# A hybrid decoder layer on one core: scratch places kept free ahead of loads, a corrected booking of products, and a new order of heads

## Chip, core and metric

The kernel runs on one core of a Trainium2 chip. The metric is the device time in microseconds (us) of one execution. The engines are named as the profile names them: PE multiplies matrices (PEld is its weight load), DVE works on vectors, ACT evaluates functions and copies, POOL fills and copies, SP issues the DMAs. Each engine takes its own instructions in the order in which they stand in the program, and waits for the others through semaphores.

## What is computed

One layer of a decoder for 272 prompt positions (16 learned ones and 256 given) and 32 sample positions (8 sequences of 4): 304 columns in all, called T. The reference, cut down:

```
xn = rms_norm(x, norm_mix)
z = xn @ w_in                        # 2048 -> 3360 (RWKV group) + 4096 (retention group)
o_a, S_a = rwkv7_mixer(z[..., :3360], ...)     # 16 heads of 64, state per head 64x64
o_b, S_b = retention_mixer(z[..., 3360:], ...) # 4 heads of 256, state per head 256x256
h = x + concat([o_a, o_b]) @ w_out
hn = rms_norm(h, norm_ffn)
h = h + (silu(hn @ w_gate) * (hn @ w_up)) @ w_down   # 2048 -> 5632 -> 2048
y = rms_norm(h, norm_final)          # meta positions dropped
```

The old states of the eight sample sequences (`state_rwkv`, `state_ret`) are read, and the new ones written.

## The kernel before

**Products.** Activations lie transposed: 128 features in the partitions, the positions in the free dimension. Each weight block of 128x128 is loaded in float32 (tile `wr`, 128x512, that is four blocks, 256 KB; five such buffers), split into a rounded part `wh` (cast on ACT) and a rest `wl` (subtraction on DVE), and multiplied in the single-pass type `float32r` with activations that are split in the same way (`xh`, `xl`): three PE instructions a block, written `acc<-xh,wh`, `acc<-xl,wh`, `acc<-xh,wl`, with 288, 290 or 304 columns. One `wr` tile therefore feeds 12 PE instructions. All weights lie in one stream `big` in the order of use.

**Stages.** First the input projection: three low-rank tiles, then for each of 8 pairs of RWKV heads (`p0` to `p7`) three tiles, for each of 4 retention heads (`r0` to `r3`) six, and for each gate (`g0` to `g3`) two. Then the output projection in two halves (`out`), the first of which needs the results of all 8 pairs, the second those of the retention heads; then the feed-forward part (from about 661 us to the end). While the products of the input run, the recurrences of the heads run as *streams*: Python generators (`pair`, `sample`, `by_token`, `ret` and others), each of which issues a few instructions and yields. They use small float32 products that go to other PSUM banks (`mm`).

**Order.** Nothing is scheduled on the chip: `Plan` walks the program once as a draft with booked durations, decides when a stream's next step is put between the products of the main stream, and the second walk emits the instructions in that order. `Plan.array` books PE's products; `Plan.book` books all others and keeps a clock for each engine. `ORDER` is the order of the heads in the input projection; `AHEAD` and `RAHEAD` say how many pairs and retention heads may be projected before earlier ones have begun; `RSTART[h]` names the pair whose end retention head h waits for; the rank with which a stream is added decides who goes first (`1 + p` for pair p, `20 + h` for retention head h; smaller goes first).

**Scratch.** All other tiles lie in two arenas in SBUF, `arena_dt.float` and `arena_dt.float32r` (so the trace names all of them alike). `Room` notes for each tile from when to when the draft uses it, and `Room.place` packs them, so that tiles of different times share a place. It tries to leave a gap of up to 2000 ns between the last use of a place and the next tile's first, and takes less where the room is short. Where a tile takes over a place, its first instruction waits for the last of the place's users. Tiles that a DMA fills are: `lora` (128x256, 128 KB, two for each pair), `s0w` (a pair's old states, 256 KB, twice for each pair), `s0r` (old retention states, 512 KB, four for each head, again four later for heads 2 and 3), `rmask` (one for each retention head) and `xT` (the residual, four loads of 576 KB in `out`).

**The DMA queue.** Loads of `wr`, loads of scratch tiles and all stores are issued by SP, one after the other. SP waits for each in its turn.

Of the kernel before, what the change touches and what calls it, by code (L numbers as in the profile page):

```python
# [47 lines left out]
WS = 5  # L48
PAIRS = 3
PMAX = 4  # L50
AHEAD = 2
RETS = 2
HELD = 2
RAHEAD = 3
RSTART = (-1, -1, 6, 6)
ORDER = "p0 p1 p2 r0 p3 p4 r1 p5 p6 p7 r2 r3 g0 g1 g2 g3"


PV = {}
# [22 lines left out]
KEYS = ((0, META, SEQ, 0), (P, P, NP - P, SEQ), (LASTK, 2 * P, T - 2 * P, SEQ + NP - P))  # L82
RMW = SEQ + NP - P + T - 2 * P
ROOM = 33008
WIDE = 4800
FREE, GAPS, TRIES = 800.0, (2000.0, 1000.0, 500.0, 200.0, 50.0, 0.0), 12


# [233 lines left out]
class Plan:  # L322
# [53 lines left out]
    def book(self, eng, what, a, k):  # L376
# [13 lines left out]
        n = math.prod(out.shape[1:])  # L390
        if eng == "PE":
            done = self.array(what, *a[:3], at) + 170
        elif eng == "SP":
            self.clock[eng] = at = max(self.clock[eng] + 400, at)
            self.dma = max(self.dma, at + 1400) + 4 * out.shape[0] * n / 320
            done = self.dma + 600
        else:
            each = sum(math.prod(x.shape[1:]) == 1 for x in ins) if n > 1 else 0
            if eng == "DVE":
                big = max(math.prod(x.shape[1:]) for x in aps)  # L400
                per = 0.56 if what == "tensor_scalar" and ins[0].name not in self.banks else 1.05
                dur, tail = {"stream_shuffle": (62 + 1.05 * n, 90), "transpose": (95 + 1.02 * n, 80), "tensor_reduce": (40 + 1.8 * big, 85),
                             "tensor_tensor_scan": (65 + 2.1 * n, 85)}.get(what, (62 + per * n + 67 * each, 83))
            elif eng == "ACT":
                dur, tail = 108 + 0.83 * n + 90 * each - 40 * (ins[0].name in self.banks), 94
            else:
                dur, tail = (60 + 0.85 * n, 60) if what == "memset" else (125 + 0.8 * n, 65) if what == "tensor_copy" else (185 + 1.65 * n, 60)
# [8 lines left out]
            done = at + tail  # L416
        for x in aps:
            for room in self.rooms.values():
                room.use(x, self.count, self.begun if eng == "PE" else self.clock[eng] - 400, done)
        for name in {x.name for x in aps if x.name in self.left}:  # L420
            self.left[name] -= 1
            assert self.left[name] >= 0, name
# [33 lines left out]
    def array(self, what, out, w, x, ready):  # L456


        n, m, k = math.prod(x.shape[1:]), math.prod(w.shape[1:]), w.shape[0]
        up = lambda v: 32 if v <= 32 else 64 if v <= 64 else 128  # L460
        mode, part = (up(k), up(m)), (w.start_partition(), out.start_partition())
        least = 110 if m > 64 else 58
        if w.dtype == F32R:
            mode = up(k), 128
            dur = max(0.417 * n + 13, 107)
        elif what == "transpose":
            dur = max(0.833 * n + 3, least)
        else:
            dur = 2 * max(0.833 * n + 3, least)
        if mode != self.mode:  # L470
            self.mode, self.parts, self.empty = mode, {}, self.clock["PE"] + 90
        at = max(self.parts.get(part, self.empty), self.begun + 5)
        self.idle += max(0.0, ready - at)
        if ready > at + 20 and w.dtype != F32R:
            dur += 90
        at = max(at, ready)
        self.begun = at
        self.parts[part] = at + dur
        self.clock["PE"] = max(self.parts.values())
        return at + dur  # L480
# [126 lines left out]
class Step:  # L607
# [389 lines left out]
    def pair_jobs(self, p):  # L997
# [10 lines left out]

        need = lambda: p < AHEAD or ("go", p - AHEAD) in self.done
        return [self.z_job(3 + 3 * p + j, post(n, 3 + 3 * p + j), need if j == 0 else None,  # L1010
# [466 lines left out]
    def ret_jobs(self, h):  # L1477
# [3 lines left out]
        r = {}  # L1481
# [23 lines left out]
        def v_post(e):  # L1505
            def f(acc):
                if e == 0:
                    r[2] = self.t([P, 2, T], "rv")
                dve.tensor_mul(r[2][:, e, :], acc[:, :T], self.rstd1)
                yield  # L1510
                if e:
                    self.plan.add(self.ret(h, r[0], r[1], r[2]), 20 + h)
            return f

        need = lambda: h < RAHEAD or ("rgo", h - RAHEAD) in self.done
        jobs = []
# [471 lines left out]
```

## Time and profile before

| what | value |
|---|---|
| median of 3 runs | 1567.01 us (1562.27 to 1572.35) |
| the profiled execution | 1565.75 us, of which its span 1563.9 us |
| PE busy | 1511.4 us (97%), 11438 instructions |
| PEld busy | 1480.9 us (95%) |
| DVE, ACT, POOL busy | 1092.1 us (70%), 881.5 us (56%), 31.5 us (2%) |
| moved by DMA | 258.57 MB, mean 165 GB/s |
| mean granted clock of PE | 0.992 |

The ends of PE's instructions are modelled in the profile, so that a busy PE isn't PE at its peak; idle time of PE and a row's count of instructions say more. "PE mm L317 <- ACT" in the rows on waits reads: PE's instruction that writes an `mm` tile waited, and ACT's instruction ended the wait. All instructions are recorded by one helper, line 317, so the rows are told apart by tiles and by time. "SPq" is the waiting of the DMA queue itself.

### The profile page before, as it was taken

The page shows a single profiled execution, that of the slowest core. Times are in us where ns is not written, and L with a number is a line of the kernel's source. Part 1 is how long each engine was busy: PE and PEld are TensorE (multiplying, and loading weights), DVE is VectorE, ACT ScalarE, POOL GpSimd, SP SyncE. Part 2 cuts the span into 40 slices and gives each one's busy share as a digit, 9 for nine tenths or more (in the row PEclk, how much of TensorE's full clock was granted, in tenths as well). Part 3 has the DMA queues.
Part 4 walks back from the last instruction along what each step waited for, and adds up shares of the span by engine and source line. Part 5 has one row for each costly group of instructions (what it writes and reads, how often), then busy time and mean ns, then how long its engine had stood idle before and what let it go on. Part 6 is the DMA issues. An engine that isn't in the chain of part 4 may idle for free.

```text
span 1563.9 us, 32063 instructions
## 1 busy us (share of the span) xinstructions
PE 1511.4 (97%) x11438; PEld 1480.9 (95%) x11438; DVE 1092.1 (70%) x2768; ACT 881.5 (56%) x2109; POOL 31.5 (2%) x165
## 2 busy tenths in 40 slices
PE   8999999999999998998999999999999999999997
PEld 7999899989899997898999999999999999999997
DVE  5988998797889755876665656565656566565657
ACT  6777678676677864556744444444444444444445
POOL 0000010000000000000000000000000000000000
PEclk9999999999999999999999999999999999999999
DMA  6454453354343345874765555555556555566554
GB/s 225 142 161 135 145 166 104 125 165 146 104 146 110 108 126 193 302 260 136 225 185 170 175 169 169 170 175 168 168 171 175 168 176 166 169 173 175 164 174 129
DMA packets 138784, 258.57 MB, mean 165 GB/s; under 512 B 16256, under 2 KB 22656, under 8 KB 138624
## 3 DMA queue, kind: packets, MB, share of 16 engines
q1 hardware_dynamic: 138624, 256.52, 53.6%
q8 instruction: 91, 1.49, 0.4%
q14 instruction: 69, 0.57, 0.1%
HBM read 242.18 MB, written 14.28 MB: 164 GB/s over the span
## 4 chain that ended last, share of the span: by engine, by line
PE 82%; DVE 6%; ACT 4%; DMA 4%; issue 2%; SPq 1%; DVEq 0%; ACTq 0%
PE acc L317 72%; PE mm L317 10%; DVE arena_dt.float L317 4%; ACT arena_dt.float L317 3%; DVE wl L317 2%; DMA arena_dt.float<-s0r 1%; ACT wh L317 1%; DMA wr<-big 1%; DMA arena_dt.float<-lora 1%; SPq L317 1%; DVE xl L317 0%; DVE arena_dt.float32r L317 0%; DMA arena_dt.float<-s0w 0%; DMA arena_dt.float<-xT 0%; ACT arena_dt.float32r L317 0%
## 5 line engine op out<-in xcount | busy, mean ns | idle before, releaser
L317 PE MATMUL acc<-xh,wh 128*128 128x288 f32 (+2 forms) x2592 | 782.9, 302 | 3.8 <-ACT wh L317 3.0
L317 PE MATMUL acc<-xh,wl 128*128 128x288 f32 (+2 forms) x2592 | 765.5, 295 | 2.9 <-DVE wl L317 2.8
L317 PE MATMUL acc<-xl,wh 128*128 128x288 f32 (+2 forms) x2592 | 761.3, 294 | 0.0
L317 ACT CAST wh<-wr 128x512 fp32r<-128x512 f32 (+1 forms) x827 | 501.0, 616 | 338.9 <-PE acc L317 268.3
L317 DVE TENSOR_TENSOR wl<-wr,wh 128x512 fp32r<-128x512 f32 (+1 forms) x827 | 560.3, 685 | 161.0 <-ACT wh L317 155.7
L317 PEld LDWEIGHTS acc<-xh,wh 128*128 128x128 f32 x2592 | 487.3, 188 | 8.7 <-ACT wh L317 4.5
L317 PEld LDWEIGHTS acc<-xh,wl 128*128 128x128 f32 x2592 | 486.2, 188 | 4.9 <-DVE wl L317 4.4
L317 PEld LDWEIGHTS acc<-xl,wh 128*128 128x128 f32 x2592 | 487.2, 188 | 3.1 <-issue 1.9
L317 PE MATMUL acc<-arena_dt.float32r,wh 128*128 128x288 f32 x1408 | 272.7, 292 | 0.2 <-DVE arena_dt.float L317 0.2
L317 PEld LDWEIGHTS acc<-arena_dt.float32r,wh 128*128 128x128 f32 x1408 | 223.7, 188 | 0.4 <-DVE arena_dt.float L317 0.4
L317 PE MATMUL acc<-arena_dt.float32r,wl 128*128 128x288 f32 x704 | 205.6, 292 | 0.0
L317 PE MATMUL mm<-arena_dt.float 128*128 128x128 f32 (+7 forms) x1120 | 171.2, 310 | 27.9 <-ACT arena_dt.float L317 11.2
L317 PEld LDWEIGHTS mm<-arena_dt.float 128*128 128x128 f32 (+1 forms) x1120 | 140.8, 184 | 43.5 <-issue 23.5
L317 DVE TENSOR_TENSOR arena_dt.float<-acc,arena_dt.float 128x288 f32<-128x288 f32 (+4 forms) x181 | 72.7, 419 | 153.3 <-PE acc L317 149.6
L317 DVE TENSOR_TENSOR arena_dt.float<-arena_dt.float 128x32 f32<-128x32 f32 (+23 forms) x658 | 159.2, 279 | 16.3 <-ACT arena_dt.float L317 6.6
L317 ACT ACTIVATE arena_dt.float<-arena_dt.float 128x288 f32<-128x288 f32 (+7 forms) x229 | 97.1, 432 | 106.5 <-DVE arena_dt.float L317 104.6
L317 DVE TENSOR_TENSOR arena_dt.float<-arena_dt.float,acc 128x288 f32<-128x288 f32 (+1 forms) x210 | 94.3, 450 | 78.9 <-PE acc L317 77.7
L317 PEld LDWEIGHTS acc<-arena_dt.float32r,wl 128*128 128x128 f32 x704 | 132.1, 188 | 0.0
L317 ACT COPY arena_dt.float<-mm 64x64 f32<-64x64 f32 (+11 forms) x338 | 95.0, 290 | 47.3 <-PE mm L317 36.0
L317 ACT CAST arena_dt.float32r<-arena_dt.float 128x288 fp32r<-128x288 f32 (+6 forms) x117 | 49.7, 430 | 93.9 <-DVE arena_dt.float L317 83.0
L317 ACT COPY arena_dt.float<-arena_dt.float 128x8 f32<-128x8 f32 (+8 forms) x267 | 62.4, 282 | 32.4 <-DVE arena_dt.float L317 27.8
L317 DVE TENSOR_TENSOR arena_dt.float32r<-arena_dt.float,arena_dt.float32r 128x288 fp32r<-128x288 f32 (+6 forms) x116 | 51.7, 448 | 5.1 <-ACT arena_dt.float32r L317 4.5
(68 smaller groups left out, 578.5 us busy)
## 6 DMA issues: line engine op xcount, KB each, us to landing
wr<-big SPq DMA_DIRECT2D x823, 256.0 KB, 2.9
arena_dt.float<-s0r SPq DMA_DIRECT2D x24, 512.0 KB, 4.5
out_rts<-arena_dt.float SPq DMA_DIRECT2D x16, 512.0 KB, 4.9
arena_dt.float<-s0w SPq DMA_DIRECT2D x16, 256.0 KB, 2.6
arena_dt.float<-xT SPq DMA_DIRECT2D x4, 576.0 KB, 4.1
arena_dt.float<-lora SPq DMA_DIRECT2D x16, 128.0 KB, 2.6
out_rws<-arena_dt.float SPq DMA_DIRECT2D x8, 256.0 KB, 4.3
out_y<-arena_dt.float SPq DMA_DIRECT2D x7, 288.0 KB, 2.4
```

Of the source, the lines that this page charges most:

```text
L317: return self._plan.keep(f(*a, **k))
```

## The change

The diff, without the parts that only move lines:

```diff
-AHEAD = 2
+AHEAD = 4
 RETS = 2
 HELD = 2
-RAHEAD = 3
-RSTART = (-1, -1, 6, 6)
-ORDER = "p0 p1 p2 r0 p3 p4 r1 p5 p6 p7 r2 r3 g0 g1 g2 g3"
+RAHEAD = 2
+RSTART = (-1, -1, 6, 5)
+RRANK = (20, 21, 22, 2.5)
+ORDER = "p0 p1 p2 r0 p3 p4 r1 g0 p5 p6 g1 p7 r2 g2 g3 r3"
...
-WIDE = 4800
+WIDE = 4288
...
         for x in aps:
             for room in self.rooms.values():
-                room.use(x, self.count, self.begun if eng == "PE" else self.clock[eng] - 400, done)
+                room.use(x, self.count, self.begun if eng == "PE" else self.clock[eng] - (8000 if eng == "SP" else 400), done)
...
         if w.dtype == F32R:
             mode = up(k), 128
-            dur = max(0.417 * n + 13, 107)
+            dur = max(0.417 * n + (9 if n == 288 else 11.5), 107)
...
-                    self.plan.add(self.ret(h, r[0], r[1], r[2]), 20 + h)
+                    self.plan.add(self.ret(h, r[0], r[1], r[2]), RRANK[h])
```

A tile that SP loads now counts as in use from 8000 ns (before: 400 ns) ahead of the booked issue of its load, so `Room.place` looks for a place whose last user is done by then. A single-pass product of 288 columns is booked at 129.1 ns (before 133.1), others 1.5 ns shorter than before. The float32r arena may take 4288 elements a partition (before 4800), and the float32 arena gets what is left of 33008. Gates are projected between pairs, retention head 3 last of all; it may begin after pair 5 (before: pair 6), and its stream goes ahead of all pairs but the first two. The set of instructions of each engine stays the same: 10841 on PE, 2650 on DVE, 2111 on ACT, 954 on SP, 169 on POOL.

What this does to the order shows at three places. The first is SP's queue at the load of the states of pair 1 (`s0w`), in the input projection; the names in brackets are the engines (or DMA queues) whose semaphore the row waits for. Before:

```order
L317 DMA wr_1473<-big 128x512 [waits DMAHW6_49,DVE_49]
L317 DMA wr_1492<-big 128x512 [waits DMAHW7_49,DVE_49]
L317 DMA arena_dt.float_73<-s0w 128x512 [waits DVE_49]
L317 DMA wr_1517<-big 128x512 [waits DMAHW0_49,Activation_49]
L317 DMA wr_1539<-big 128x512 [waits DMAHW1_49,Activation_49]
```

The changed kernel:

```order
L318 DMA wr_1510<-big 128x512 [waits DMAHW0_49,DVE_49]
L318 DMA wr_1530<-big 128x512 [waits DMAHW1_49,DVE_49]
L318 DMA arena_dt.float_73<-s0w 128x512
L318 DMA wr_1558<-big 128x512 [waits DMAHW2_49,DVE_49]
L318 DMA wr_1578<-big 128x512 [waits DMAHW3_49,DVE_49]
```

The load stands at nearly the same place in the queue, but no longer waits for DVE: the last user of its place is 138 PE instructions earlier in the program, where before it was the same step of the pair's own stream. Of the 64 loads of scratch tiles, 49 stood before within 60 PE instructions after the last use of their place, and 26 within 10; now 18 and 7 do.

The second place is SP's queue where the input projection ends and `out` begins: the old states (`s0r`) of retention heads 2 and 3. Before:

```order
L317 DMA arena_dt.float_73<-s0r 128x1024 [waits DMAHW3_49,Pool_49]
L317 DMA arena_dt.float_73<-s0r 128x1024 [waits DMAHW4_49]
L317 DMA arena_dt.float_73<-s0r 128x1024 [waits DMAHW5_49,DMAHW1_49,PE_49]
L317 DMA arena_dt.float_73<-s0r 128x1024 [waits DMAHW6_49,DMAHW2_49,PE_49]
L317 DMA arena_dt.float_73<-s0r 128x1024 [waits DMAHW7_49,DMAHW3_49,PE_49]
L317 DMA arena_dt.float_73<-s0r 128x1024 [waits DMAHW4_49,DMAHW0_49,PE_49]
L317 DMA wr_8040<-big 128x512
```

The changed kernel:

```order
L318 DMA arena_dt.float_73<-s0r 128x1024 [waits DVE_49,DMAHW5_49,PE_49,Activation_49]
L318 DMA arena_dt.float_73<-s0r 128x1024 [waits DMAHW6_49]
L318 DMA arena_dt.float_73<-s0r 128x1024 [waits DMAHW7_49]
L318 DMA arena_dt.float_73<-s0r 128x1024 [waits DMAHW0_49]
L318 DMA arena_dt.float_73<-s0r 128x1024 [waits DMAHW1_49,Pool_49]
L318 DMA arena_dt.float_73<-s0r 128x1024 [waits DMAHW2_49,Pool_49]
L318 DMA arena_dt.float_73<-xT 128x4x288 [waits DMAHW5_49,PE_49,DMAHW6_49,Activation_49,Pool_49]
```

Before, the second four loads waited for PE's products of the same two heads, into whose places they went. Now one wait for an engine that has a near user is left among them, the first row's, for the last steps of pair 6.

The third place is PE at the same point. `mm` rows of 128x128 by `cst` are transposes of retention heads; 32x256 is a product with the old states; the rows of 128x288 with `float32r` are the last products of a pair; the first `acc` row opens `out`. Before:

```order
L317 MATMUL acc_7876<-xh_75,wl_7769 128x288
L317 MATMUL mm_1945_7913<-arena_dt.float_73 128x256 x2
L317 MATMUL mm_1954_7941<-arena_dt.float_73 128x256 x6
L317 MATMUL mm_1955_7954<-arena_dt.float_73 128x256 x6
L317 MATMUL mm_1956_7962<-arena_dt.float32r 128x288 x4
L317 MATMUL mm_1959_7968<-arena_dt.float_73 32x256 x8
L317 MATMUL mm_1964_7981<-arena_dt.float_73 32x256 x8
L317 MATMUL mm_1975_8033<-arena_dt.float_73 128x256
L317 MATMUL acc_7876<-xh_75,wh_7790 128x288
```

The changed kernel:

```order
L318 MATMUL acc_7784<-xh_75,wl_7788 128x304
L318 MATMUL mm_1926_7894<-arena_dt.float_73 128x128 x8
L318 MATMUL mm_1931_7909<-cst_323,arena_dt.float_73 128x128 x4
L318 MATMUL mm_1936_7936<-arena_dt.float32r 128x288 x4
L318 MATMUL mm_1943_7955<-arena_dt.float32r,sums_326 128x288 x2
L318 MATMUL mm_1948_7974<-arena_dt.float32r,sums_326 128x288 x2
L318 MATMUL mm_1956_7984<-arena_dt.float_73 32x256 x8
L318 MATMUL mm_1975_8054<-arena_dt.float32r 128x288 x4
L318 MATMUL mm_1982_8080<-arena_dt.float_73 32x256 x8
L318 MATMUL acc_8100<-xh_75,wh_7817 128x288
```

(Rows between these are left out.) Before, the last weight products of the input ran until only the four last products of pair 7 were left, and 76 instructions of heads 2 and 3 and of pair 7 stood between them and `out`. Now 102 stand there, among them the whole end of pair 7, from its eight output products (`mm_1926`) over its two sums (`sums`) to its last four products (`mm_1975`), with head 3 between them; part of head 2 has moved behind the start of `out`.

## Prediction

> **What bounds the kernel now.** I read the page first:
>
> ```profile
> PE 1511.4 (97%) x11438; PEld 1480.9 (95%) x11438; DVE 1092.1 (70%) x2768; ACT 881.5 (56%) x2109; POOL 31.5 (2%) x165
> ```
>
> PE bounds the kernel: its instructions stay the same, so only the time in which it stands still, or runs slowly, can change: 1563.9 - 1511.4 = 52.5 us. The Trainium skill ("Trainium Kernel Development and Optimization", Performance Expectations) says that weight-load busy time, not matmul busy time, tells the distance from the limit. By that the room is 1563.9 - 1480.9 = 83.0 us; the row shows both, and I use the smaller one below, as what a wait can surely give back.
>
> Next, where it stands still, by stretches (columns: length, busy time of each engine with its instructions, granted clock, DMA share, GB/s):
>
> ```profile
> core 0: us, PE busy (x) PEld busy (x) DVE busy (x) ACT busy (x) POOL busy (x), PEclk, DMA share, GB/s
> ...
> 100.00:200.00 100.00, 93.90 (x700) 89.57 (x698) 90.29 (x382) 66.38 (x200) 5.78 (x30) 1.00 0.47 152
> 200.00:300.00 100.00, 95.29 (x723) 93.15 (x722) 82.79 (x253) 78.08 (x236) 5.47 (x28) 1.00 0.38 116
> 300.00:400.00 100.00, 93.93 (x688) 89.43 (x687) 83.48 (x296) 74.59 (x217) 4.43 (x25) 0.98 0.48 152
> 400.00:500.00 100.00, 93.86 (x698) 92.24 (x697) 89.49 (x354) 67.14 (x200) 6.60 (x32) 0.98 0.38 120
> ...
> 576.20:587.10 10.90, 10.90 (x82) 9.35 (x84) 7.00 (x18) 6.42 (x19) 0.21 (x1) 1.00 0.25 98
> 587.10:598.20 11.10, 7.03 (x45) 2.55 (x36) 1.29 (x3) 0.44 (x2) 0.00 (x0) 0.70 0.73 263
> 598.20:602.10 3.90, 3.90 (x30) 3.75 (x29) 0.00 (x0) 1.66 (x4) 0.00 (x0) 0.98 0.03 6
> 602.10:661.00 58.90, 53.42 (x390) 51.56 (x390) 50.27 (x104) 33.85 (x73) 0.00 (x0) 1.00 0.75 253
> ...
> 722.00:775.00 53.00, 47.47 (x318) 42.51 (x317) 31.28 (x61) 39.26 (x129) 1.38 (x7) 1.00 0.53 167
> 775.00:1500.00 725.00, 725.00 (x5627) 725.00 (x5626) 437.60 (x786) 313.28 (x547) 0.00 (x0) 1.00 0.59 173
> ```
>
> From 775 us on PE never waits: 5627 instructions in 725 us, 128.8 ns each. The change leaves that part alone. PE's idle time lies in the input projection (6.1 + 4.7 + 6.1 + 6.1 = 23.0 us from 100 to 500 us), at the turn to `out` (587 to 598 us), in `out` (5.5 us from 602 to 661) and where the late new states of the pairs run beside the first feed-forward products (5.5 us from 722 to 775).
>
> Then what PE waits for there, and what SP did just before. Each pair of rows below is one short window, in order of time (103 to 118, 168 to 180, 277 to 296, 322 to 333, 357 to 369, 408 to 424, 424 to 433, 485 to 496 us): first PE's wait, then SP's (us in total, times, longest):
>
> ```profile
> PE mm L317 <- ACT arena_dt.float L317: 1.6, 1, 1.6
> SPq L317 <- DVE arena_dt.float L317: 8.7, 2, 7.2
> ...
> PE mm L317 <- issue: 1.5, 1, 1.5
> SPq L317 <- ACT arena_dt.float L317: 5.8, 1, 5.8
> ...
> PE mm L317 <- POOL arena_dt.float L317: 1.4, 1, 1.4
> PE mm L317 <- ACT arena_dt.float L317: 0.9, 1, 0.9
> SPq L317 <- DVE arena_dt.float L317: 19.8, 2, 11.2
> ...
> PE mm L317 <- issue: 0.9, 1, 0.9
> SPq L317 <- ACT arena_dt.float L317: 9.0, 1, 9.0
> ...
> PE mm L317 <- ACT arena_dt.float L317: 2.4, 1, 2.4
> SPq L317 <- DVE arena_dt.float L317: 8.1, 1, 8.1
> ...
> PE mm L317 <- DVE arena_dt.float L317: 2.3, 1, 2.3
> SPq L317 <- DVE arena_dt.float L317: 9.6, 2, 7.2
> ...
> PE mm L317 <- issue: 1.2, 1, 1.2
> SPq L317 <- DVE arena_dt.float L317: 10.5, 1, 10.5
> ...
> PE mm L317 <- issue: 1.1, 1, 1.1
> SPq L317 <- ACT arena_dt.float L317: 5.4, 1, 5.4
> ```
>
> This is what to see: PE's rows name ACT, DVE, POOL or nothing ("issue"), but ahead of each stall SP stood 5 to 11 us at one scratch load, because the place that it fills was still in use. Everything behind it in the queue came late: five `wr` tiles in a burst, or a `lora` tile. Then ACT, which casts both in its order, waited for the landing, and with it the small copies that PE needed:
>
> ```profile
> ACT wh L317 <- DMA wr<-big: 4.1, 1, 4.1
> ...
> ACT arena_dt.float32r L317 <- DMA arena_dt.float<-lora: 3.4, 1, 3.4
> ```
>
> The first is from 408 to 424 us, the second from 424 to 433. Five `wr` tiles hold 5 x 12 products, 7.7 us at 128.8 ns: about as long as SP stood.
>
> **Term 1, these eight stalls.** They sum to 1.6 + 1.5 + 2.3 + 0.9 + 2.4 + 2.3 + 1.2 + 1.1 = 13.3 us. Two of them cost more than their length:
>
> ```profile
> 368.00:374.00 6.00, 5.00 (x26) 5.01 (x27) 3.31 (x10) 3.95 (x16) 0.00 (x0) 0.72 0.96 325
> 423.00:429.00 6.00, 5.98 (x37) 5.98 (x38) 5.27 (x21) 5.36 (x17) 0.21 (x1) 0.72 0.00 0
> ```
>
> Right after the stalls of 2.4 and 2.3 us the granted clock has a mean of 0.72 over 6 us: (1 - 0.72) x 6 = 1.7 us of PE's work each, 3.4 us. (The Trainium skill, "TensorE: Matmul & The Clock Gate", HAM oscillation, has PE's clock fall only after idle gaps above about 3.4 us. By that rule these two stalls would leave the clock alone and this term would be 3.4 us less; the two rows show that 2.3 us was enough here.) So 16.7 us hang on blocked loads. Of the loads within 10 PE instructions after their place's last use 7 of 26 remain (within 60, 18 of 49), so I leave 30% of the stalls: a gain of **11.7 us**, between 0 and 16.7. What hides a load then is the distance itself. What is late next is ACT and DVE at their own work, which is rival A.
>
> **Term 2, the turn to `out`.** Around 587 us SP shows one wait:
>
> ```profile
> SPq L317 <- PE mm L317: 11.2, 1, 11.2
> ```
>
> This is the second four `s0r` loads, 2 MB, which could go out only when PE had read the first ones. PE then had nothing else: from 587.1 to 598.2 us it ran 45 instructions, and at clock 0.70. The same kind ran before at this rate:
>
> ```profile
> 585.61 1.93 PE L317 MATMUL mm<-arena_dt.float 128*32 128x256 f32 x32
> ```
>
> 45 of them are 2.7 us, so 11.1 - 2.7 = 8.4 us are lost. In the new order the wait for PE on these loads is gone, but for one row, behind the end of pair 6. Against that, pair 7's end now has no weight products beside it. From its eight output products to its last four lies a chain of some 17 dependent steps on ACT and DVE, each of about 0.44 us; with 0.1 us to hand over that is 9 us (an estimate from rows of the next kind):
>
> ```profile
> 579.15 0.44 ACT L317 ACTIVATE arena_dt.float<-arena_dt.float 128x288 f32<-128x288 f32 x1
> ```
>
> Between these two PE has 24 transposes and most of head 3 and a part of head 2. From the 10.9 us that a like set took from 576.2 to 587.1, less what has moved behind, more the transposes, I estimate 13 us of PE work. So the chain fits, if ACT and DVE serve it at once; they also have the copies of heads 2 and 3. I charge 3 us for that: a gain of **5.4 us**. Bounds: 8.4 if nothing of the chain shows; -3 in rival B.
>
> **Term 3, `out`.** 58.9 - 53.4 = 5.5 us idle. SP's longest wait stands at the residual's load:
>
> ```profile
> SPq L317 <- DVE xl L317: 15.5, 1, 15.5
> ```
>
> The changed kernel still waits for PE at this load, the eight `s0r` loads of the held heads come a little earlier, and the bytes are the same in a stretch with the DMA engines at 0.75. I take half, **2.7 us**, between 0 and 5.5.
>
> **Term 4, the late states.** 53.0 - 47.5 = 5.5 us idle, and
>
> ```profile
> SPq L317 <- PE mm L317: 18.9, 5, 5.1
> ```
>
> Of the eight `s0w` loads here four still wait for PE in the new order (before, five did), but between a transpose and the 128x512 product that follows, 33 to 42 weight products stand in most cases, where 27 to 30 stood. Eight more are 1 us each. I take half: **2.8 us**, between 0 and 5.5.
>
> **Term 5, the rest.** From 100 to 500 us 23.0 - 13.3 = 9.7 us of idle time are not tied to loads. The new order deals these waits anew. It also has more distance for tiles that no DMA writes: 32 of them, before 127, are within 10 PE instructions after another engine's use of their place. The shorter booking puts 4 ns more cover on each 288-column product: in 48 such products 0.2 us, no term of its own. I take **2 us**, from -8 to +8: a new order may bring as many waits as it takes away, but hardly twice as many.
>
> **Sum.** 11.7 + 5.4 + 2.7 + 2.8 + 2 = 24.6 us. The profiled execution took 1565.75 us, 1.9 us beside its span, and 1.3 us less than the median shown. 1565.75 - 24.6 = **1541 us**, 1.6% faster. About 1% is what a measurement of this kernel can tell from no change: below 1551 us is faster, above 1583 us slower. With all terms at their best (16.7 + 8.4 + 5.5 + 5.5 + 8 = 44.1) it is 1522 us.
>
> **Rival A: ACT and DVE take over the stalls (about 1556 us, within 1%).** DVE is busy for 90.3 of the 100 us from 100 to 200, and 89.5 from 400 to 500. PE's work there would come faster while DVE's stays, so a blocked load may only have been the last of several late things. If half of terms 1 and 3 is real and the others give nothing but 3 us of the turn, the sum is 5.9 + 1.4 + 3 = 10 us. Against it: ACT's waits for `wr` and `lora` name the DMA itself. Here too belongs that the change doesn't do what it says: the 8000 ns are a wish that gives way where the room is short, and 18 loads still stand near. That gives the same size. Chance 0.24.
>
> **Rival B: the end of pair 7 stands bare (slower).** Before, the chain from the eight output products (563.7 us) to the last four (584.8 us) took 21.1 us, with 12.5 us of full PE work beside its first half. If it takes 21.1 us again, as ACT and DVE first serve head 3, whose stream now goes ahead of pair 7's, PE stands for 21.1 - 13 = 8 us, in gaps that halve the clock as after the stalls above (two at 1.7 us), and term 2 is -3 us, not +5.4. By itself that makes only 1549 us. It ends on the slower side if the same rank does so all through pairs 5 to 7, which head 3's weight products must cover: the bare chain and the waits of term 5 at -8, and terms 1, 3 and 4 at nothing, is 1565.75 + 3 + 8 = 1577 us or somewhat more. The point from which it decides: terms 1, 3 and 4 below 11 us together. Chance 0.06, half of that over the 1% line.
>
> **How the numbers follow.** The forecast has 0.70: faster by over 1%, between 1522 and 1551 us. Rival A has 0.24 and B 0.06. The range must leave out no more than 0.2: from 1524 us, where nearly all terms are at their best (some 0.06 lies below), to 1561 us, which takes in A's value with half of its own spread (some 0.12 lies above). Faster by over 1%: 0.70, within 1%: 0.26, slower: 0.04.
>
> **What would show it.** Term 1: between 100 and 500 us SP's waits for `arena_dt.float` fall to a third, ACT's waits for `wr` to a few us, PE's idle time from 23 to about 11 us, no clock below 1. Term 2: PE's idle time between the last input product and `out` under 4 us, and no wait for `s0r`; if A is right, PE's waits name ACT and DVE with no SP wait before them, and their sum stays above 16 us. If B is right, the stretch before `out` holds long waits of PE for ACT or DVE, with a halved clock. The prediction is wrong if blocked loads vanish and PE's idle time doesn't.

## The result

The changed kernel takes **1528.26 us** (median of 4, 1527.69 to 1529.31), the kernel before took 1567.37 us beside it (median of 4, 1562.27 to 1572.35). The ratio is 0.9751, 95% interval 0.972 to 0.9783: 39 us faster, where the forecast was 25 us, to 1541. The profiled execution took 1529.31 us, with a span of 1527.4. The helper that records every instruction is line 318 now. Where some executions of a kernel took over 1.5% longer than its fastest, its ratio is that of the others, and its median that of all.

The row of the changed kernel's page that answers to that of before, the busy times:

```profile
PE 1496.6 (98%) x11438; PEld 1474.8 (97%) x11438; DVE 1086.4 (71%) x2768; ACT 884.1 (58%) x2109; POOL 30.6 (2%) x165
```

PE's idle time went from 52.5 us to 1527.4 - 1496.6 = 30.8 us, 21.7 less. Its busy time went from 1511.4 to 1496.6 us, 14.8 less, with the same instructions.

Both profiles hold 11438 rows of PE, so a stretch that counts the same number of them ends at the same place of the work, but for what the new order has swapped around that place. I cut both spans after 100, 3701, 4801 and 5738 instructions of PE; one that lies across a cut is counted on both sides (columns: stretch, length, busy time and count of PE, PEld, DVE, ACT, POOL, granted clock, DMA share, GB/s). The kernel before:

```profile
0.00:22.90 22.90, 18.22 (x100) 15.55 (x101) 13.37 (x28) 15.52 (x32) 0.60 (x8) 0.93 0.81 262
22.90:529.80 506.90, 483.62 (x3603) 469.76 (x3601) 434.32 (x1535) 364.36 (x1065) 28.03 (x146) 0.99 0.44 136
529.80:686.70 156.90, 147.27 (x1102) 138.91 (x1102) 107.01 (x228) 93.57 (x225) 1.46 (x4) 0.98 0.63 215
686.70:819.90 133.20, 127.67 (x939) 122.71 (x939) 87.51 (x167) 80.26 (x207) 1.38 (x7) 1.00 0.60 182
819.90:1563.90 744.00, 734.59 (x5702) 734.00 (x5700) 449.93 (x814) 327.79 (x584) 0.00 (x0) 1.00 0.57 169
```

The changed kernel:

```profile
0.00:19.90 19.90, 16.02 (x100) 14.37 (x101) 12.68 (x27) 14.36 (x30) 6.13 (x41) 1.00 0.87 280
19.90:503.20 483.30, 474.64 (x3603) 466.07 (x3602) 431.70 (x1533) 362.62 (x1054) 21.78 (x114) 1.00 0.49 146
503.20:650.30 147.10, 143.91 (x1103) 137.90 (x1102) 107.14 (x231) 95.40 (x238) 1.36 (x3) 1.00 0.67 220
650.30:783.00 132.70, 127.19 (x940) 122.32 (x939) 87.38 (x167) 79.77 (x207) 1.31 (x7) 1.00 0.61 185
783.00:1527.40 744.40, 734.88 (x5702) 734.09 (x5700) 447.53 (x814) 331.99 (x584) 0.00 (x0) 1.00 0.58 169
```

So the 36.5 us between the spans are 3.0 at the start, **23.6 in the input projection** (506.9 to 483.3), **9.8 at the turn and in `out`** (156.9 to 147.1), 0.5 where the late states run, and nothing in the rest of the feed-forward stage (-0.4). In the projection PE's idle time fell from 23.3 to 8.7 us, by 14.6, and the busy time of its instructions by 9.0. The granted clock explains some 6.6 of the 14.8 us of busy time. Before, it cost (1 - 0.93) x 22.9 = 1.6 us at the start, 3.4 us after two stalls and (1 - 0.70) x 11.1 = 3.3 us at the turn; in the changed kernel one stretch is left, (1 - 0.83) x 10 = 1.7 us. Where the rest of the busy time went is not shown.

The stretches of the input projection that answer to those of before:

```profile
100.00:200.00 100.00, 94.64 (x707) 90.53 (x705) 91.03 (x374) 68.57 (x203) 2.98 (x16) 1.00 0.49 152
200.00:300.00 100.00, 99.68 (x756) 97.68 (x757) 85.26 (x286) 79.53 (x239) 6.48 (x33) 0.99 0.48 149
300.00:400.00 100.00, 97.88 (x755) 96.31 (x754) 92.63 (x308) 78.60 (x232) 6.18 (x33) 1.00 0.45 135
400.00:500.00 100.00, 99.15 (x772) 98.95 (x771) 93.57 (x397) 71.38 (x212) 4.96 (x27) 1.00 0.48 137
```

PE stands idle for 5.4 + 0.3 + 2.1 + 0.9 = 8.7 us there, before 23.0. DVE is busier than before in all four (91.0, 85.3, 92.6 and 93.6 against 90.3, 82.8, 83.5 and 89.5): it gets more done in the same time, and hasn't become the limit. What PE still waits for in these 400 us:

```profile
PE mm L318 <- ACT arena_dt.float L318: 4.2, 4, 2.8
PE mm L318 <- issue: 3.7, 3, 2.1
PE mm L318 <- DVE arena_dt.float L318: 0.6, 1, 0.6
```

These are 8 waits with 8.5 us. The kernel before had 23 with 22.5 us there.

The waits behind it, from 100 to 500 us. Of the kernel before, SP's waits for scratch tiles, and ACT's for landings (us in total, times, longest):

```profile
SPq L317 <- DVE arena_dt.float L317: 164.6, 60, 11.2
...
SPq L317 <- ACT arena_dt.float L317: 30.7, 9, 9.0
...
ACT wh L317 <- DMA wr<-big: 17.9, 8, 4.1
ACT arena_dt.float32r L317 <- DMA arena_dt.float<-lora: 7.8, 4, 3.4
```

Of the changed kernel:

```profile
SPq L318 <- DVE arena_dt.float L318: 150.1, 72, 8.0
...
SPq L318 <- ACT arena_dt.float L318: 11.4, 4, 7.9
...
ACT arena_dt.float32r L318 <- DMA arena_dt.float<-lora: 7.8, 4, 3.0
```

ACT's wait for late `wr` tiles, 17.9 us in 8 pieces, has no row any more: the queue behind a blocked load comes in time. Its waits for `lora` tiles stay as they were, 7.8 us in 4 pieces. SP itself still waits 150 us for DVE, in more and shorter pieces. That queue waits by design, and the sum of its waits says little about PE.

### The profile page after: what moved, and what is told of

Same layout as the page of the kernel before. It is cut to its first block, busy times and chain, and to the rows that moved or that the text cites. A ratio compares the mean times of both kernels' runs of the same rounds, so it can differ in the third digit from the quotient of the medians.

```text
span 1527.4 us, 31997 instructions
## 1 busy us (share of the span) xinstructions
PE 1496.6 (98%) x11438; PEld 1474.8 (97%) x11438; DVE 1086.4 (71%) x2768; ACT 884.1 (58%) x2109; POOL 30.6 (2%) x165
## 4 chain that ended last, share of the span: by engine, by line
PE 92%; DVE 3%; ACT 2%; DMA 1%; issue 1%; SPq 0%; DVEq 0%; ACTq 0%
PE acc L318 82%; PE mm L318 11%; DVE arena_dt.float L318 2%; ACT arena_dt.float L318 1%; DVE wl L318 1%; DMA wr<-big 1%; ACT wh L318 0%; DMA arena_dt.float<-xT 0%; SPq L318 0%; DMA arena_dt.float<-s0r 0%; DVE arena_dt.float32r L318 0%; ACT arena_dt.float32r L318 0%; DVE xl L318 0%; DMA arena_dt.float<-lora 0%; ACT xh L318 0%
## 5 line engine op out<-in xcount | busy, mean ns | idle before, releaser
L318 DVE TENSOR_TENSOR arena_dt.float<-acc,arena_dt.float 128x288 f32<-128x288 f32 (+4 forms) x181 | 72.7, 419 | 149.9 <-PE acc L318 147.1
L318 PE MATMUL mm<-arena_dt.float 128*128 128x128 f32 (+6 forms) x1120 | 164.0, 300 | 15.3 <-issue 9.0
L318 DVE TENSOR_TENSOR arena_dt.float<-arena_dt.float 128x32 f32<-128x32 f32 (+22 forms) x658 | 159.9, 279 | 14.2 <-ACT arena_dt.float L318 8.8
L318 PEld LDWEIGHTS mm<-arena_dt.float 128*128 128x128 f32 (+1 forms) x1120 | 138.8, 182 | 25.2 <-issue 13.7
L318 ACT COPY arena_dt.float<-mm 64x64 f32<-64x64 f32 (+10 forms) x338 | 94.8, 289 | 59.0 <-PE mm L318 50.6
L318 ACT COPY arena_dt.float<-arena_dt.float 128x32 f32<-128x32 f32 (+8 forms) x267 | 62.3, 283 | 26.1 <-DVE arena_dt.float L318 22.1
L318 DVE TENSOR_TENSOR arena_dt.float32r<-arena_dt.float,arena_dt.float32r 128x288 fp32r<-128x288 f32 (+6 forms) x116 | 52.1, 452 | 18.5 <-ACT arena_dt.float32r L318 18.1
```

The source lines that it names most:

```text
L318: return self._plan.keep(f(*a, **k))
```

## How the experiments are read

Two numbers are read from each profile, because the whole time mixes them. The first is **the point**: the time at which PE has issued 5738 or 5739 instructions, when the late states are done and only the rest of the feed-forward stage is left. It is 819.9 us before and 783.0 us in the changed kernel. The second is the count of feed-forward products in the 400 us from 900 to 1300 us. Of before and of the changed kernel:

```profile
900.00:1300.00 400.00, 400.00 (x3105) 400.00 (x3105) 239.05 (x428) 173.54 (x304) 0.00 (x0) 1.00 0.58 170
```

```profile
900.00:1300.00 400.00, 400.00 (x3105) 400.00 (x3105) 240.09 (x435) 174.91 (x301) 0.00 (x0) 1.00 0.59 171
```

That is one product every 128.8 ns. In some of the other kernels only 3002 fit, one every 133.2 ns, with PE waiting for nothing and the clock at 1.00 all the same. From the point to the end it is 744 us in the first case and 769 in the second, **25 us that have nothing to do with places**. Which of the two the profiled execution has is told with each run. The point isn't quite free of the rate, since products of this kind run ahead of it too, and it is read from one execution of each kernel.

"Near" is counted in the program, as in the section on the change: loads of scratch tiles that stand within 30 PE instructions after the last use of their place (of 64), and tiles that an engine writes within 10 after another engine's use. Before it is 40 and 127, in the changed kernel 14 and 32.

## Experiments with the order of before

**Only loads far.** The arenas as in the change, but a place is sought at a distance only for tiles that SP loads (12 and 140 near):

```diff
-WIDE = 4800
+WIDE = 4288
...
+            want = gap if i in self.loads else 0.0
...
-                    if free >= gap:
+                    if free >= want:
```

> The kernel before with every engine's instructions in the same order; only the places in scratch differ (float32r arena of 4288, and a gap ahead is sought for tiles that a DMA fills, none for the others). Loads within 60 PE instructions after their place's last use: 15 of 64 (before 49); other tiles within 10 after another engine's use: 140 (before 127). Theory L (blocked loads are what stalls PE): terms 1 and 3 and the 8.4 us of the turn, about 20 us faster than before, 1540 to 1552 us, and SP's waits for scratch fall to a third. Theory P (any tile that takes over a place too soon costs, loads or not): at most half of that, 1555 to 1562. Theory O (the new order of heads itself makes the gain): as before, 1563 to 1570.

1550.21 us, ratio 0.9899 (0.9884 to 0.9914). Its stages, cut at the same counts:

```profile
0.00:23.10 23.10, 20.03 (x100) 17.37 (x101) 13.14 (x28) 15.52 (x32) 0.60 (x8) 0.85 0.81 256
23.10:522.20 499.10, 481.92 (x3603) 468.20 (x3601) 433.29 (x1534) 364.71 (x1065) 28.61 (x147) 1.00 0.46 139
522.20:674.10 151.90, 145.59 (x1103) 139.67 (x1102) 107.36 (x229) 93.76 (x225) 1.30 (x3) 0.99 0.66 221
674.10:803.90 129.80, 127.02 (x939) 122.41 (x939) 87.09 (x167) 79.84 (x207) 1.43 (x7) 1.00 0.65 187
```

Against before that is 7.8 us in the projection, 5.0 at the turn and in `out`, 3.4 in the late states: 16.0 us at the point (803.9). Moving loads alone is worth this much, with the instruction order of before. It lies in the range of theory L, but below the 20 us that L said.

**Only the split of the arenas.**

```diff
-WIDE = 4800
+WIDE = 4288
```

> The kernel before with the float32r arena of 4288 alone; the same order of instructions. The packing then finds more distance for all tiles: 21 of 64 loads within 60 PE instructions, 80 other tiles within 10. Theory L: as the kernel with far loads alone, within 5 us of it, 1543 to 1553. Theory P: clearly faster than that kernel, by 8 us or more, 1535 to 1545. Theory O: as before, 1563 to 1570.

1553.36 us, ratio 0.9924 (0.9906 to 0.9943). By the whole time that is a third of the gain. The two numbers tell otherwise:

```profile
0.00:782.60 782.60, 766.25 (x5738) 745.03 (x5739) 639.26 (x1955) 553.42 (x1526) 30.40 (x165) 1.00 0.55 170
900.00:1300.00 400.00, 400.00 (x3003) 400.00 (x3002) 233.95 (x419) 167.75 (x294) 0.00 (x0) 1.00 0.58 165
```

The point comes at 782.6 us, as early as in the changed kernel (783.0), and the 25 us are lost later, at the slower product rate. The lower limit on the one arena leaves more room to the other, and the planner deals the same order with 11 and 80 near. The time falls into none of the three ranges because of that rate; the point, 21.3 us ahead of e1's, speaks for theory P.

**All far, order of before.** The split, a finer list of gaps with more tries, and a lead of 2000 ns for loads (8 and 37 near):

```diff
-FREE, GAPS, TRIES = 800.0, (2000.0, 1000.0, 500.0, 200.0, 50.0, 0.0), 12
+FREE, GAPS, TRIES = 800.0, (2000.0, 1700.0, 1400.0, ..., 200.0, 100.0, 0.0), 60
...
-... self.clock[eng] - 400, done)
+... self.clock[eng] - (2000 if eng == "SP" else 400), done)
```

> The kernel before with the same order of instructions, but places as far as the packing can make them: float32r arena of 4288, a lead of 2000 ns for loads, finer steps of the gap and more tries. 14 of 64 loads within 60 PE instructions and 37 other tiles within 10 (the changed kernel: 18 and 32). Theory P (places make the gain, for all tiles): within 8 us of the changed kernel, 1528 to 1537 us. Theory O2 (the new order makes the rest, once the places are far): 10 to 18 us slower than the changed kernel, 1538 to 1548. Theory L (loads alone): as the two kernels with far loads, 1548 to 1555.

1523.68 us, ratio 0.9731 (0.9718 to 0.9743): all of the gain without the new order of heads, and 4 us below the range of theory P.

```profile
0.00:22.00 22.00, 17.84 (x100) 15.89 (x101) 13.16 (x28) 15.80 (x32) 6.05 (x40) 0.92 0.84 273
22.00:508.80 486.80, 478.97 (x3602) 467.81 (x3601) 430.59 (x1532) 364.30 (x1064) 22.39 (x115) 1.00 0.47 142
508.80:654.20 145.40, 142.50 (x1103) 138.02 (x1102) 107.50 (x231) 94.11 (x225) 1.31 (x3) 1.00 0.69 231
654.20:780.80 126.60, 126.42 (x940) 122.15 (x939) 87.25 (x167) 80.02 (x207) 1.38 (x7) 1.00 0.64 192
```

Against e1, with the same instruction order, the projection gives 12.3 us more, the turn and `out` 6.5, the late states 3.2, the start 1.1. What changed between the two is mostly where tiles that engines write lie (140 near, now 37), and a little the loads (12, now 8). The number of such tiles is no measure by itself, though: from 140 to 37 the point gains 23.1 us, but from 80 (the split alone) to 37 it gains only 1.8.

**The first load alone.** Before, the first `xT` load waited for the place of ACT's `warm` tile, and was issued at 2.25 us instead of 0.73.

```diff
-        warm = self.t([P, 1], "warm")
+        warm = self.t([P, 1], "warm", pool=self.cp)
```

> The kernel before with one tile moved out of scratch: the single column that ACT writes at the start, on whose place the first load of x waited 1.6 us. All else stands near as before. If that wait sets the start: 1.5 to 3 us faster than before; if the start is hidden behind the first weights: no difference.

1578.24 us, ratio 1.0075 (1.0056 to 1.0094): slower by 12 us, though its first 40 us hold 21 PE instructions more than those of before (224).

```profile
0.00:40.00 40.00, 36.03 (x245) 33.39 (x246) 25.41 (x45) 26.95 (x51) 0.60 (x8) 1.00 0.72 237
...
0.00:825.20 825.20, 783.65 (x5739) 753.94 (x5740) 643.14 (x1955) 554.86 (x1526) 31.53 (x165) 0.99 0.51 161
665.00:715.00 50.00, 50.00 (x377) 50.00 (x377) 35.95 (x69) 27.06 (x54) 0.00 (x0) 1.00 0.72 238
900.00:1300.00 400.00, 400.00 (x3069) 400.00 (x3068) 237.39 (x424) 171.10 (x299) 0.00 (x0) 1.00 0.58 169
```

The kernel before, in the third of these stretches:

```profile
665.00:715.00 50.00, 50.00 (x390) 50.00 (x389) 37.08 (x72) 27.16 (x56) 0.00 (x0) 1.00 0.72 233
```

The order is that of before, and so are the places: the planner gives every other tile the same offset in its arena, with 40 and 127 near. So the start's 3 us are real, but by the point 5.3 us are lost on balance, and places can't be the reason. PE stood idle for 825.2 - 783.7 = 41.6 us up to the point, a little less than before (43.1). Its busy time is 6.9 us longer, and one source shows: from 665 to 715 us 377 products went through where before had 390, so the slower rate was there ahead of the point already. After the point the rate lay in between. With order and places as they were, 3 us gained at the start became 5.3 lost at the point, so single edits can't be priced more finely than some 8 us.

## Experiments with the new order

**Everything near.** The changed kernel, without looking for any distance (41 and 145 near):

```diff
-FREE, GAPS, TRIES = 800.0, (2000.0, 1000.0, 500.0, 200.0, 50.0, 0.0), 12
+FREE, GAPS, TRIES = 800.0, (0.0,), 12
```

> The changed kernel with the same order of instructions, but no gap sought for any tile: 48 of 64 loads within 60 PE instructions, 145 other tiles within 10, as near as before the change. Theory L: it loses the load terms, about 20 us, 1543 to 1553. Theory P: loses 25 us or more, 1553 to 1567. Theory O: stays at 1527 to 1533.

1601.34 us, ratio 1.0206 (1.014 to 1.0272), slower than any of the three theories said. Two executions took 1591.5 and 1591.7 us, two 1611.0 and 1616.8. The last of these was profiled and has the slower rate:

```profile
0.00:846.30 846.30, 788.78 (x5738) 757.28 (x5739) 645.22 (x1955) 553.03 (x1526) 31.53 (x165) 0.98 0.51 157
900.00:1300.00 400.00, 400.00 (x3002) 400.00 (x3001) 233.84 (x422) 168.74 (x291) 0.00 (x0) 1.00 0.58 165
```

The point lies 63.3 us behind that of the changed kernel, whose order of instructions is the same. With near places the new order is worse than the old one, by 26.4 us. A part of the 63.3 us is the halved clock: its mean up to the point is 0.98 here.

**Only loads far, new order** (the edit of e1's `want` in the changed kernel; 10 and 138 near):

> The changed kernel with the same order of instructions, a gap sought for loaded tiles alone: 14 of 64 loads within 60 PE instructions, 138 other tiles within 10 (the changed kernel: 18 and 32). Theory L: as the changed kernel, 1526 to 1533. Theory P: slower by 8 us or more, 1536 to 1550. Theory O: 1527 to 1533.

1574.53 us, ratio 1.0057 (1.0042 to 1.0072).

```profile
0.00:803.30 803.30, 774.03 (x5739) 747.89 (x5740) 642.79 (x1955) 552.03 (x1526) 31.77 (x165) 0.99 0.55 166
900.00:1300.00 400.00, 400.00 (x3002) 400.00 (x3002) 231.98 (x416) 169.34 (x293) 0.00 (x0) 1.00 0.57 165
```

43.0 of the 63.3 us are back at the point; the slower rate hides it in the whole time, which lies outside the ranges of all three theories. Of what is missing, one piece is again a load: from 160 to 178 us PE's longest wait and SP's are

```profile
PE mm L318 <- ACT arena_dt.float L318: 4.3, 1, 4.3
...
SPq L318 <- DVE arena_dt.float L318: 15.2, 2, 14.6
```

SP stood 14.6 us at an `s0r` load of the first retention head, one of the 10 that are left near. Five `wr` loads went out in a burst behind it, ACT waited 3.8 us for one of them, and PE for ACT. The stalls forecast for before look just like this.

**Only engines' tiles far, new order** (the reverse: `want = 0.0 if i in self.loads else gap`; 19 and 37 near):

> The changed kernel, but the gap is sought only for tiles that an engine writes; tiles that SP loads take the lowest free place. Of the loads of 64 instructions or less after the last use of their place there are 31 within 60 matrix products (18 in the changed kernel), while engine-written tiles stay far (37 against 32). If near places of the loads cost what the old order gave back when they were made far (16 us in e1), this run is at 1528 + 8 to 16 = 1536 to 1545 us, with waits of SP for arena tiles that end in idle time of TensorE in the input projection. If the engine-written tiles are what matters, within 8 us of the changed kernel: 1520 to 1536 us. Forecast: 1536, so close to the border; above 1540 speaks for the loads, below 1532 for the engine-written tiles.

1539.41 us, ratio 0.9812 (0.9788 to 0.9836), so on the border, as forecast. Four executions took 1532 to 1540 us, two 1562 and 1566; one of these two was profiled, at the slower rate. By the point it is clear that the near loads cost something, 8.0 us against the changed kernel:

```profile
0.00:791.00 791.00, 769.66 (x5738) 746.68 (x5739) 638.30 (x1955) 552.53 (x1526) 30.92 (x165) 0.99 0.54 168
900.00:1300.00 400.00, 400.00 (x3002) 400.00 (x3002) 231.44 (x415) 169.55 (x294) 0.00 (x0) 1.00 0.56 165
```

55.3 of the 63.3 us. So in the new order loads alone give 43.0 and engines' tiles alone 55.3, together 63.3: the two overlap. The edit doesn't part them cleanly either, since with far places for the one kind fewer of the other stand near too (19 loads, not 41).

**The order alone** (`AHEAD`, `RAHEAD`, `RSTART`, `RRANK`, `ORDER`; the split, the lead and the booking as before; 9 and 28 near):

> The change of the order alone (ORDER, AHEAD, RAHEAD, RSTART, RRANK): lead 400 ns, float32r arena 4800, products booked as before. Its packing comes out far by itself: 21 loads within 60 PE instructions, 28 other tiles within 10. Theory P: 1528 to 1538 us, nearly the whole gain. If the lead or the booking makes the gain: 1548 or more.

1524.46 us, ratio 0.9726 (0.9709 to 0.9743), the gain without the three other edits, and more than theory P said (one of the four executions took 1549.07):

```profile
0.00:779.20 779.20, 765.92 (x5738) 743.30 (x5739) 637.96 (x1955) 552.49 (x1526) 30.42 (x165) 0.99 0.55 171
```

**Without the lead** (8000 ns back to 400; 9 and 39 near) and **without the new booking** (`0.417 * n + 13` again; 8 and 34 near), all other edits as changed:

> The changed kernel with the lead put back to 400 ns; same order of instructions, other places: 18 loads within 60 PE instructions and 39 other tiles within 10 (32 with the lead). Theory P: the lead is worth next to nothing, 1526 to 1532 us. If the lead is what keeps SP free: 1538 to 1550.

> The changed kernel with the old booking of one-pass products of 288 columns (13 ns more than the columns' time, not 9), so that the third part of the change is undone alone; order and lead stay. The places come out slightly farther (11 loads within 60 products against 18, 34 engine-written tiles within 10 products against 32). If the gain lies in the places and the booking matters only through them: 1520 to 1532 us, the same as the changed kernel. If the truer booking itself brings instructions to better moments: 1535 to 1550 us.

Without the lead the kernel had two kinds of executions, at 1514.48 and 1516.14 us (ratio 0.9674, 0.9657 to 0.969) and at 1539.53 and 1543.02; the median of 1527.83 lies between them, and in the range of theory P by that alone. The second kind was profiled:

```profile
0.00:772.50 772.50, 762.27 (x5739) 743.33 (x5740) 637.36 (x1955) 552.23 (x1526) 30.79 (x165) 1.00 0.56 172
900.00:1300.00 400.00, 400.00 (x3002) 400.00 (x3002) 232.79 (x420) 168.81 (x291) 0.00 (x0) 1.00 0.56 165
```

Without the booking it took 1543.53 us, ratio 0.9855 (0.9839 to 0.9871):

```profile
0.00:771.50 771.50, 762.91 (x5739) 742.02 (x5740) 638.17 (x1955) 552.67 (x1526) 30.77 (x165) 1.00 0.55 172
900.00:1300.00 400.00, 400.00 (x3002) 400.00 (x3001) 235.35 (x422) 166.64 (x291) 0.00 (x0) 1.00 0.56 165
```

The second range, which was to speak for the booking, holds this time, but only by the slower rate. At the point both kernels are ahead of the changed one, by 10.5 and 11.5 us, so neither edit adds to the gain. Without the lead the order of the instructions stays and only places move. Without the booking it does not stay, other than the expectation says: the old booking also changes the draft, and all engines' instructions stand in the order of the kernel with the order alone (e6). Of the three kernels, that with all four edits has the most near loads (14 against 9 and 8).

**A finer list of gaps** in the changed kernel, with the lead at 400 ns (6 and 40 near), twice:

> The changed kernel with more steps in the list of gaps (fourteen from 2000 ns to 0), 60 tries, and the lead of a load at 400 ns: a candidate for the best of both. Loads within 60 / 30 / 10 products of the last use of their place: 9/6/2 (18/14/7 in the changed kernel); engine-written tiles within 5 / 10: 23/40 (21/32). If the places of loads still cost something in the changed kernel (four stalls of 4 to 8 us on SP's queue are left): 1515 to 1522 us. If what is left is in the engine-written tiles, or nothing: 1524 to 1532 us. Forecast: 1520.

> The kernel with the finer list of gaps (fourteen steps, 60 tries) and the lead at 400 ns once more, unchanged. In its profile the matrix products of the feed-forward stage came every 133.33 ns at a granted clock of 1.00 with nothing waited for, those of the changed kernel every 128.89 ns; over the 5,700 products from there to the end that is 25 us, and all of its times lay at 1538 to 1540. If the rate goes with the kernel (the moment at which its stage begins), every time is again 1537 to 1541 us. If it goes with the execution or the chip, some or all of the times are at 1539 less 25 = 1512 to 1516 us, and the kernel is then 13 us faster than the changed one. Up to the 5,700th product from the end nothing may change: 769 us, 14 us before the changed kernel's 783. Forecast: both levels appear.

1538.88 us, ratio 0.9825 (0.9811 to 0.984), and on another chip 1538.08, 0.9821 (0.9797 to 0.9845). The first one's profile:

```profile
0.00:769.30 769.30, 760.87 (x5739) 742.12 (x5740) 638.24 (x1956) 551.66 (x1526) 31.00 (x165) 1.00 0.56 173
900.00:1300.00 400.00, 400.00 (x3002) 400.00 (x3001) 233.73 (x421) 168.77 (x292) 0.00 (x0) 1.00 0.57 165
```

It has the earliest point of all, 13.7 us ahead of the changed kernel (767.5 us on the other chip), and the slower rate in all of 11 executions, so that as a whole it is slower, 19 us over the 1520 of the forecast. The expectation that both levels appear was wrong: here the rate went with the kernel. What such a point gives at the faster rate shows in the kernel without the lead, at 1514 and 1516 us.

All runs in one view; point and product are those of the profiled execution. For e3, e7 and e9 that was a longer one, and the medians are over all executions:

| kernel | near: loads, others | point, us | product, ns | median, us |
|---|---|---|---|---|
| before | 40, 127 | 819.9 | 128.8 | 1567.4 |
| old order, loads far (e1) | 12, 140 | 803.9 | 128.8 | 1550.2 |
| old order, split alone (e2) | 11, 80 | 782.6 | 133.2 | 1553.4 |
| old order, all far (e5) | 8, 37 | 780.8 | 128.8 | 1523.7 |
| old order, first load free (e8) | 40, 127 | 825.2 | 130.3 | 1578.2 |
| new order, all near (e3) | 41, 145 | 846.3 | 133.2 | 1601.3 |
| new order, loads far (e4) | 10, 138 | 803.3 | 133.2 | 1574.5 |
| new order, others far (e9) | 19, 37 | 791.0 | 133.2 | 1539.4 |
| **changed** | 14, 32 | 783.0 | 128.8 | 1528.3 |
| order alone (e6) | 9, 28 | 779.2 | 128.8 | 1524.5 |
| no lead (e7) | 9, 39 | 772.5 | 133.2 | 1527.8 |
| no booking (e10) | 8, 34 | 771.5 | 133.2 | 1543.5 |
| finer gaps (e11) | 6, 40 | 769.3 | 133.2 | 1538.9 |

Among the six kernels of the new order whose engines' tiles lie far (e6 and e10 in one order of instructions, the four others in another), the point follows the loads within 30: 6, 8, 9, 9, 14, 19 stand at 769.3, 771.5, 772.5, 779.2, 783.0, 791.0 us. Over the whole range that is some 1.7 us for each, but the two with 9 are 6.7 us apart. Counted within 60, as in the prediction, they are 9, 11, 18, 21, 18, 31, and the rule has an exception. So it is a tendency, and no price.

## Why the prediction was right, and where it wasn't

The direction, the cause and the range held; the size was short by 14 us, most of it in the input projection.

- **Term 1 (11.7 us) and term 5 (2 us)**, the input projection: 13.7 forecast, 23.6 measured. The mechanism of term 1 stands: ACT's waits for `wr` are gone, PE's idle time is 8.7 us (11 forecast), and e1, which moves loads alone, gives 7.8 us in this stage (term 1 said 11.7) and 16.0 in all where terms 1 to 4 said 22.6. Late `lora` tiles, which the prediction held against the same queue, still cost ACT as much as before. The mis-sized step is term 5. "Tiles that no DMA writes" were put down at 2 us, with 8 as the most; e5 against e1 gave 23.1 us over all stages, 12.3 of them here. The prediction counted the tiles (127, then 32) and gave the number no price. It also looked for the gain where PE stands idle: of the 23.6 us here 9.0 are busy time, for which it had only the clock after two stalls, 2.4 us (70% of 3.4). Its opening sum, 1563.9 - 1511.4 = 52.5 us, holds idle time alone, not that in which PE runs slowly, as its sentence says. How a near place of that kind costs PE its time was not shown: that a short wait on ACT or DVE delays all that stands behind it, the last user of the next load's place among it, is argued only. How the 23 us divide between such waits and the last near loads stays open too, since e4 and e9 overlap.
- **A marker was wrong.** "SP's waits for scratch fall to a third" holds for those that ACT ended (30.7 to 11.4 us), not for DVE's (164.6 to 150.1). And the clock still fell once, after PE's longest wait of 2.8 us:

```profile
196.00:206.00 10.00, 7.23 (x45) 6.99 (x44) 8.25 (x31) 5.42 (x17) 0.52 (x1) 0.83 0.67 215
```

- **Terms 2 and 3 (5.4 + 2.7)**, the turn and `out`: 8.1 forecast, 9.8 measured. PE is idle for 25.20 - 23.89 = 1.3 us at the turn, under the 4 us forecast, and 1.2 us of waits for `s0r` are left in two pieces, where the marker said none: SP still stood 13.2 us at these loads, for DVE. Pair 7's bare chain shows in no row of waits, so rival B has nothing. PE came to the pair's last four products 18.5 us after its first output product (549.2 and 567.7 us) and was busy for all of that but some 1.2 us, where the prediction estimated 13 us of work.

```profile
547.00:572.20 25.20, 23.89 (x183) 19.94 (x182) 14.46 (x35) 16.52 (x44) 0.58 (x1) 1.00 0.55 207
...
PE mm L318 <- DMA arena_dt.float<-s0r: 1.2, 2, 0.7
```

- **Term 4 (2.8 us)**, the late states: 0.5 measured. PE still waits there for nothing that the profile names, 5.4 us in four pieces from 700 to 745 us. That this stage can be had is seen in e5 (126.6 us, before 133.2).
- **The start** (3.0 us) was in no term. The first load's wait for `warm` stood in the trace, and I didn't read the first 3 us.
- **Rival A** would have left PE waiting for ACT and DVE in place of loads, at 1556 us. It fell: DVE went up to 93.6 of 100 us and PE's idle time went down, to waits of 8.5 us where A's marker was a sum above 16.
- **What no rival held** is the product rate. The last 744 us were taken as fixed. They were the same in both kernels, but seven of the other kernels show that this was luck: at the slower rate the changed kernel would have been at 1528 + 25 = 1553 us.

What is shown of the change is one thing. Each of two edits gives the planner enough room to put tiles far from their last users: the split alone (37.3 us at the point) and the order alone (40.7). All four together give 36.9. Whether the new order is also worth something by itself stays open. With places about as far, the old order has its point at 780.8 us (e5; 8 and 37 near), the new ones at 772.5 and 771.5 (e7; 9 and 39, e10; 8 and 34). These 8 to 9 us are no more than the 10.5 us by which two dealings of one order differ (e7 and the changed kernel).

## What to carry to other kernels

When scratch memory is reused by plan, price every tile whose place was used shortly before, those that engines write as well as those that are loaded: here the places alone, with the same instructions in the same order, moved the point by 63 us (a far place also has another address; that the address plays no part was not tested apart). An edit that re-deals the places is judged by the dealing that comes out, so compare several dealings before any one edit is given the credit, and look whether it changes the order too. And compare kernels at a fixed place of the work as well as by the whole time: a later stage that falls into another rate can hide the whole effect, as it did in e2.

## What was not expected of the hardware

Feed-forward products of 288 columns come at one of two steady rates, both at a granted clock of 1.00 and with no wait in the trace: 3105 or 3002 of them in 400 us, 128.8 or 133.2 ns each, 744 or 769 us from the point to the end. Where it is slow, it is so from where the small products of the late states end, some 730 to 810 us, to the end, also where PE's last idle gap lies long before (606 us with the finer gaps). In the kernel e8 it was there from 665 to 715 us too, and after the point lay between, with 3069. Some kernels had only one (the finer gaps the slower, 11 of 11; the change the faster, 4 of 4), others both, by execution, as without the lead. The kernel before had the faster one in its profile, but of its 39 executions beside the experiments 6 took 1589.6 to 1594.9 us, some 25 us more than the others, as the slower rate would make it; none of these was profiled. The booking before, 0.417 x 288 + 13 = 133.1 ns, is the one rate, the booking of the change, 129.1 ns, the other, but the rate doesn't follow the booking (e2 has the old one and e4 the new one, both at 133.2 ns). What picks the rate is open: it is not the order of the work (e1 and e2 have the same), not order and places together (e8 has those of before), and not the granted clock.

Idle gaps of 2.3 to 2.8 us were enough for the granted clock to fall, before (two) and after (one). The Trainium skill ("TensorE: Matmul & The Clock Gate", HAM oscillation) has it fall after gaps above about 3.4 us; here shorter ones were enough, and no run shows that bound.
